# First loads in one queue with the tokens ahead of the adaLN blocks, and two tiles entering the first FFN at once, chunk by chunk

## Chip, cores, metric

One Trainium2 chip, one program on 8 cores (two dies, cores 0 to 3 and 4 to 7). The metric is the device time of the slowest core in microseconds (us). A second, slower state occurs in some executions: one die has a lower granted TensorE clock (the share of its full clock that the chip let TensorE have) and the time is some per cent longer. The ratios leave such runs out and compare fast runs with fast runs; the medians given in us are over all runs of a kernel, so they are only a rough guide.

## The reference, cut to what matters

Two layers of a diffusion backbone. Each sub-layer modulates its input by shift, scale and gate that come out of a matrix product with the conditioning vector (adaLN). The first thing that happens to the tokens is:

```python
mod = silu(cvec) @ ada_w[0] + ada_b[0]             # shift, scale, gate of three sub-layers
h = rms_norm(x, norm_g) * (1 + scale) + shift      # first norm
x = x + 0.5 * gate * ((silu(h @ w1_gate) * (h @ w1_up)) @ w2)
... convolution and attention mixer, FFN; then layer 1 (pooling mixer); final norm
```

Each core has 1280 tokens of width 1024, in tiles 0 and 1 (512 tokens each) and tile 2 (256). So before the first useful matmul a core needs tokens (tile 0: 2 MB), the adaLN blocks for shift and scale (8 of 1 MB) and W1 (22 blocks of 1 MB, gate and up columns side by side).

## The kernel before

A small list scheduler written in Python takes threads of operations, estimates when each could start, and fixes the order on every engine before the program is built. At run time each engine works through its list in that fixed order and waits on semaphores. The ring is a set of buffers through which all weight blocks pass; PSUM banks are the memory that TensorE writes its sums to; the entry is the stretch in which a tile's first W1 matmuls follow its normalisation chunk by chunk (128 channels each). Cuts are marked `...`; comments that explain the code were added here.

```python
IN = [(ACT, True), (DVE, True)] * 4      # squares on ScalarE and VectorE; each summed over channels by an fp32 matmul with ones
A8 = [(ACT, False)] * 8                  # squares on ScalarE, added up on VectorE, ONE fp32 matmul at the end

def xload(self):                         # sync queue
    yield from self.xtile(0, SP)         # tile 0: two loads of 1 MB
    yield self.wait("xin")
    ...                                  # six small loads: finalg, convw, pscale, qkg, amask, cmask

def seq():                               # order of blocks on the GpSimd queue
    for i in range(4):
        yield from ada(0, 4 + i, 5 + i)  # scale block
        yield from ada(0, i, i + 1)      # shift block
    a = list(w1(0, 0))
    yield from a[0:6]
    yield from mix(a[6:], ada(0, 8, 24))
...
for key, src, shape in seq():
    if key in (("w1", 0, 0, 2), ("w1", 0, 0, 3)):
        yield from self.xtile(key[3] - 1, POOL)      # tiles 1 and 2
        self.sigl("xin")
    if key == ("ada", 0, 8):                         # conditioning rows, on the sync queue,
        for v in range(2):                           # into two free slots of the ring: 512 KB each
            ...
            yield self.dma(SP, self.ring[slot[1]][:, :].bitcast(F32),
                           self.d_crow[v:v + 1, :].broadcast_to([128, 1024]), ...)
    ...

# entry of a tile into W1, in ffn(): two W1 blocks (4 PSUM banks), channel chunk by channel chunk
if j == 0 and ("w1", l, s, 1) in self.W:
    ...
    for c in range(8):
        yield self.wait(("h", t, l, i), c + 1)
        yield self.mm([... for q in range(4)], ...)
    ...
norms(1, 0, 0, [IN] * 3)
```

The first eight adaLN blocks are multiplied on TensorE (16 tiny matmuls a block); later ones are dot products on VectorE with the conditioning rows.

The softmax here doesn't subtract the row's maximum and nothing guards it: scores larger than these inputs give would overflow.

## Time and profile before

| | value |
|---|---|
| time, median of 4 runs | 1447.47 us (1446.47 lowest; one slow run of 1593.38) |
| profiled execution | another execution, slow on die 1 (1478.4 us); cores 0 to 3 undisturbed |
| TensorE busy, share of the span | 97% |
| chain that ended last, TensorE's share | 93% |

The cores of the profiled execution of the kernel before: core, span, mean granted clock.

```profile
core 0: 1443.7 us, clock 0.990
core 1: 1439.5 us, clock 0.993
core 2: 1444.4 us, clock 0.994
core 3: 1438.8 us, clock 0.992
...
die 1 (median of its cores): 1472.6 us, clock 0.971
```

Die 1 is in the slow state, so everything below is read from core 0 (or cores 0 to 3).

The chain of waits of core 0 over the first 110 us, in order of time: start, duration, what. This shows what ended the start.

```profile
2.59 33.76 DMA sb_xres<-xin
...
37.14 7.04 PE ps L298 x24
...
51.87 1.38 ACT sb_hbuf L314 x2
53.26 0.53 ACT sb_sq L314
...
53.92 56.16 PE ps L298 x281
```

Tile 0 takes until 36.4 us to arrive.

TensorE of core 0 in the kernel before, in order of time: start, duration, operation, count, and in brackets the idle time before it. `sb_sq,sb_onesf` are the fp32 sums of squares (a matmul appears as two records), `sb_scb` the adaLN matmuls, `sb_hbuf,sb_ring` the W1 matmuls.

```profile
44.00 2.14 PE L298 MATMUL ps<-sb_scb,sb_ring 128*128 128x2 bf16 x80
47.10 5.93 PE L298 MATMUL ps<-sb_hbuf,sb_ring 128*128 128x512 bf16 x20 [0.96 <-issue]
53.92 1.96 PE L298 MATMUL ps<-sb_sq,sb_onesf 128*128 128x512 f32 x4 [0.89 <-ACT sb_sq L314]
...
63.45 12.32 PE L298 MATMUL ps<-sb_hbuf,sb_ring 128*128 128x512 bf16 x56
75.61 1.03 PE L298 MATMUL ps<-sb_sq,sb_onesf 128*128 128x256 f32 x4
```

Between 53.92 and 63.45 us the sums of tile 1 alternate with W1 matmuls of tile 0. At 75.61 us tile 2's fp32 sums begin (8 matmuls of 0.43 us).

### The profile page before, as it was taken

The numbers are of one execution on the slowest core, as the hardware profiler recorded it, in microseconds if no ns is written. First come the engines' busy times: TensorE is split into PE (matmuls) and PEld (weight loads), VectorE is DVE, ScalarE is ACT, GpSimd is POOL, SyncE is SP. The second block draws the span as 40 slices with busy tenths as digits, with TensorE's granted clock in tenths as the row PEclk, the third lists the DMA queues.
The fourth block names the chain that finished last, engine by engine and source line by source line (L and its number), as shares of the span: only waits on it lengthen the run. The fifth ranks groups of instructions, "written<-read, shape, count | busy, mean of one in ns | idle before, by whom it ended". The sixth has DMA issues, their size and how long they took to land.

```text
span 1476.5 us, 21048 instructions; the slowest of 8 cores (1438.8 to 1476.5 us)
## 1 busy us (share of the span) xinstructions
PE 1427.4 (97%) x8578; PEld 774.1 (52%) x8578; DVE 827.6 (56%) x1479; ACT 508.1 (34%) x826; POOL 176.0 (12%) x298
## 2 busy tenths in 40 slices
PE   2899999999999999999999999999999999999997
PEld 0455555457644554555554655555546746555445
DVE  0478861156757998888764478742244862122234
ACT  0651111034399977311123331111133771111111
POOL 3011111334210101111100021100000101000000
PEclk9999999999999999999999999999999999999998
DMA  9999972002629725499750089863221376330012
GB/s 176 215 161 167 151 118 45 15 11 46 99 48 144 116 44 95 74 167 161 119 98 3 1 133 172 152 104 68 44 45 30 55 117 114 59 67 5 1 57 86
DMA packets 42047, 132.19 MB, mean 90 GB/s; under 512 B 6368, under 2 KB 9184, under 8 KB 41952
## 3 DMA queue, kind: packets, MB, share of 16 engines
q0 software_dynamic: 34272, 120.42, 49.2%
q1 hardware_dynamic: 7680, 10.44, 2.3%
q8 instruction: 67, 1.10, 0.3%
q14 instruction: 28, 0.23, 0.1%
HBM read 241.55 MB, written 6.55 MB: 168 GB/s over the span
## 4 chain that ended last, share of the span: by engine, by line
PE 93%; DMA 3%; DVE 1%; ACT 1%; issue 0%; SPq 0%; POOL 0%; DVEq 0%; another core or an unknown queue 0%; ACTq 0%
PE ps L298 93%; DMA sb_xres<-xin 2%; DMA sb_ring<-adaw 1%; DVE sb_nt L319 1%; ACT sb_sg L314 0%; PE ps L307 0%; ACT sb_hbuf L314 0%; ACT sb_areg L314 0%; DVE sb_areg L324 0%; ACT sb_acc L314 0%; DMA yo<-sb_nt 0%; SPq L349 0%; ACT sb_sq L314 0%; DVE sb_xres L319 0%; DVE sb_ring L648 0%
## 5 line engine op out<-in xcount | busy, mean ns | idle before, releaser
L298 PE MATMUL ps<-sb_hbuf,sb_ring 128*128 128x512 bf16 (+1 forms) x4512 | 860.2, 353 | 2.1 <-issue 1.0
L298 PEld LDWEIGHTS ps<-sb_hbuf,sb_ring 128*128 128x128 bf16 x4512 | 446.3, 100 | 391.3 <-issue 89.3
L298 PE MATMUL ps<-sb_areg,sb_ring 128*128 128x512 bf16 (+1 forms) x2304 | 426.1, 345 | 0.0
L314 ACT ACTIVATE sb_sg<-ps 128x512 f32<-128x512 f32 (+3 forms) x279 | 146.1, 528 | 547.2 <-PE ps L298 509.4
L298 PEld LDWEIGHTS ps<-sb_areg,sb_ring 128*128 128x128 bf16 x2304 | 224.3, 98 | 190.8 <-issue 8.3
L324 DVE TENSOR_TENSOR sb_areg<-ps,sb_sg 128x512 bf16<-128x512 f32 (+1 forms) x264 | 157.8, 601 | 297.1 <-PE ps L298 286.8
L319 DVE SCALAR_TENSOR_TENSOR sb_xres<-ps,sb_gsc,sb_xres 128x512 f32<-128x512 f32 (+1 forms) x152 | 96.7, 650 | 165.0 <-PE ps L298 164.4
L648 DVE CUSTOM_DVE_ANT_0 sb_sq<-sb_ring,sb_crow,sb_adab 128x1024 bf16<-128x1024 bf16 x128 | 163.8, 1280 | 23.0 <-DMA sb_ring<-adaw 20.7
L648 DVE CUSTOM_DVE_ANT_0 sb_ring<-sb_ring,sb_crow,sb_adab 128x1024 bf16<-128x1024 bf16 x128 | 163.9, 1280 | 1.9
L314 ACT ACTIVATE sb_sq<-sb_xres 128x512 f32<-128x512 f32 (+1 forms) x123 | 67.9, 558 | 278.7 <-DVE sb_xres L319 217.1
L319 DVE SCALAR_TENSOR_TENSOR sb_nt<-sb_xres,sb_asc,sb_acc 128x512 f32<-128x512 f32 (+1 forms) x144 | 90.5, 664 | 13.8 <-ACT sb_acc L314 10.2
L314 ACT ACTIVATE sb_hbuf<-sb_nt,sb_modsb 128x512 bf16<-128x512 f32 (+1 forms) x136 | 85.4, 659 | 34.0 <-DVE sb_nt L319 33.7
L349 POOL DMA_DIRECT2D sb_ring<-w1t x88 | 47.4, 552 | 349.6 <-PE ps L298 206.4
L324 DVE TENSOR_TENSOR sb_acc<-sb_acc,sb_sq 128x512 f32<-128x512 f32 (+1 forms) x105 | 64.0, 611 | 38.3 <-ACT sb_sq L314 37.7
L349 POOL DMA_DIRECT2D sb_ring<-adaw x72 | 38.7, 540 | 344.1 <-PE ps L298 200.7
L314 ACT ACTIVATE sb_sg<-ps,sb_amask 128x1024 bf16<-128x1024 f32 x67 | 72.7, 1119 | 5.0 <-PE ps L298 4.7
L298 PE MATMUL ps<-sb_areg 128*128 128x65 bf16 (+3 forms) x568 | 60.1, 272 | 3.5 <-ACT sb_sg L314 2.3
L298 PE MATMUL ps<-sb_sq,sb_onesf 128*128 128x512 f32 (+1 forms) x60 | 28.4, 598 | 22.9 <-DVE sb_sq L324 11.5
L349 POOL DMA_DIRECT2D sb_ring<-w2t x44 | 23.3, 529 | 215.1 <-PE ps L298 160.7
L298 PEld LDWEIGHTS ps<-sb_areg 128*128 128x128 bf16 (+1 forms) x568 | 27.8, 95 | 38.9 <-issue 22.8
L218 ACT ACT_TABLE_LOAD x36 | 46.2, 1283 | 1.4 <-PEq L282 0.7
L298 PE MATMUL ps<-sb_ring,sb_hbuf 128*128 128x256 bf16 x320 | 38.6, 276 | 0.2
(75 smaller groups left out, 462.1 us busy)
## 6 DMA issues: line engine op xcount, KB each, us to landing
sb_ring<-w1t POOLq DMA_DIRECT2D x88, 512.0 KB, 13.8
sb_ring<-adaw POOLq DMA_DIRECT2D x72, 512.0 KB, 10.2
sb_ring<-w2t POOLq DMA_DIRECT2D x44, 512.0 KB, 6.3
sb_areg<-mp POOLq DMA_DIRECT2D x5, 512.0 KB, 8.6
sb_xres<-xin SPq DMA_DIRECT2D x2, 1024.0 KB, 26.1
sb_xres<-xin POOLq DMA_DIRECT2D x2, 1024.0 KB, 43.0
sb_ring<-wcx POOLq DMA_DIRECT2D x4, 512.0 KB, 10.9
sb_ring<-wo POOLq DMA_DIRECT2D x4, 512.0 KB, 9.7
```

The costliest lines, as they stand in the source:

```text
L218: eng.preload_act_table_set(ACT_SETS[tab])
L298: ins = e.matmul(m[0], lhsT=m[1], rhs=m[2], start=m[3], stop=m[4], **({"skip_group_check": True} if len(m) > 5 else {}))
L314: o = Op(ACT, lambda e: e.activation(out=out, in_=in_, func=func, **kw), reads, writes, cost)
L319: return Op(DVE, lambda e: e.scalar_tensor_tensor(out=out, in0=in0, scalar=scalar, in1=in1, op0=op0, op1=op1), reads, writes, 150.0 + 1.04 ...
L324: return Op(eng, lambda e: e.tensor_tensor(out=out, in0=in0, in1=in1, op=op), reads, writes, c)
L349: return Op(q, lambda e: e.dma_start(out=out, in_=in_), reads, writes, 600.0 if q == POOL else 450.0, True, nbytes, key)
L648: return Op(DVE, lambda e: e.tensor_tensor_reduce(out=prod, in0=w, in1=self.crow[:, v, :], scale=1.0, scalar=bias, op0=ALU.mult, op1=ALU.a ...
```

## The change

Its intent: all big first loads go into the GpSimd queue in the order of need (tile 0, four adaLN blocks, tile 1, two blocks, W1 0 and 1, two blocks, W1 2, tile 2). Tile 1 enters W1 at the same time as tile 0, in a thread of its own and with one W1 block, so TensorE has matmuls of two tiles while the last adaLN blocks are on their way. Tile 2's squares are added on VectorE.

```diff
     def xload(self):
-        yield from self.xtile(0, SP)
         yield self.wait("xin")
 ...
         def seq():
+            a = list(w1(0, 0))
             for i in range(4):
+                if i == 3:
+                    yield from a[0:2]
                 yield from ada(0, 4 + i, 5 + i)
                 yield from ada(0, i, i + 1)
-            a = list(w1(0, 0))
-            yield from a[0:6]
+            yield from a[2:6]
 ...
+        yield from self.xtile(0, POOL)
         for key, src, shape in seq():
-            if key in (("w1", 0, 0, 2), ("w1", 0, 0, 3)):
-                yield from self.xtile(key[3] - 1, POOL)
+            if key in (("ada", 0, 6), ("w1", 0, 0, 3)):
+                yield from self.xtile(1 if key[0] == "ada" else 2, POOL)
                 self.sigl("xin")
 ...
             if j == 0 and ("w1", l, s, 1) in self.W:
 ...   (the old entry, written in place)
+                nj = 1 if (l, s, t) == (0, 0, 1) else 2
+                room(t, nj - 1)
+                todo[t] += nj
+                if (l, s) == (0, 0):
+                    S.spawn(entry(t, nj), 5.5)      # both tiles at once
+                else:
+                    yield from entry(t, nj)
 ...
+        yield Wait(lambda: not any(left.values()))
         self.sigl(("w1done", l, s))
 ...
-        norms(1, 0, 0, [IN] * 3)
+        norms(1, 0, 0, [IN, IN, A8])
```

The wait before `w1done` makes sure that the entries, now threads of their own, are over. A new field that can delay an operation in the scheduler's estimate is also added, but nothing sets it.

More of the change, by code (lines that the diff above doesn't have):

```diff
@@ L49 @@
     __slots__ = ("eng", "fn", "reads", "writes", "cost", "is_dma", "nbytes", "key", "deps", "marked", "sig", "dval",
-                 "t_end", "tab", "p")
+                 "t_end", "tab", "p", "after")
     def __init__(self, eng, fn, reads, writes, cost, is_dma=False, nbytes=0, key=None):
@@ L58, in __init__ @@
         self.p = None
+        self.after = 0.0
         self.sig = 0
@@ L136, in est @@
     def est(self, o):
-        t = self.free[o.eng]
+        t = max(self.free[o.eng], o.after)
         for d in self.deps_of(o):
@@ L858, in done1, with entry @@
                 self.wfree(("w1", l, s, j))
+        def entry(t, nj):
+            c0, n, v = TILES[t]
+            ks = []
+            for q in range(2 * nj):
+                k = yield from self.bank()
+                ks.append(k)
+            Wv = [self.W[("w1", l, s, q)] for q in range(nj)]
+            for c in range(8):
+                yield self.wait(("h", t, l, i), c + 1)
+                yield self.mm([(self.psv(ks[q], n), Wv[q // 2][0][:, c, 128 * (q % 2):128 * (q % 2) + 128],
+                                self.hbuf[:, c, c0:c0 + n], c == 0, c == 7) for q in range(2 * nj)],
+                              [w[1] for w in Wv] + [self.bh[t][c]], [self.psb[k] for k in ks])
+            for q in range(nj):
+                done1(q)
+                S.spawn(evac(ks[2 * q], ks[2 * q + 1], t, q, n), 1)
         while sum(todo.values()) < 3 * NJ:
@@ L864, in ffn @@
             if j == 0 and ("w1", l, s, 1) in self.W:
-                room(t, 1)
-                todo[t] += 2
-                ks = []
-                for q in range(4):
-                    k = yield from self.bank()
-                    ks.append(k)
-                Wv = [self.W[("w1", l, s, q)] for q in range(2)]
-                for c in range(8):
-                    yield self.wait(("h", t, l, i), c + 1)
-                    yield self.mm([(self.psv(ks[q], n), Wv[q // 2][0][:, c, 128 * (q % 2):128 * (q % 2) + 128],
-                                    self.hbuf[:, c, c0:c0 + n], c == 0, c == 7) for q in range(4)],
-                                  [Wv[0][1], Wv[1][1], self.bh[t][c]], [self.psb[k] for k in ks])
-                for q in range(2):
-                    done1(q)
-                    S.spawn(evac(ks[2 * q], ks[2 * q + 1], t, q, n), 1)
+                nj = 1 if (l, s, t) == (0, 0, 1) else 2
[5 more added lines that the diff above has]
+                    yield from entry(t, nj)
                 continue
```

## The prediction

> What bounds the kernel now. The page gives TensorE 97% of the span, and the chain of waits is 93% TensorE. The profiled run is in the slow state on die 1, so I read cores 0 to 3 (spans 1438.8 to 1444.4 us, clock 0.99). By stretches, TensorE is fully busy from about 75 us on; no wait of it is listed between 100 and 260 us. So only the first 75 us can be shortened; there the DMA share is about 1.0.
>
> The start (transfers' landing, core 2). Token tile 0 comes on the sync queue and shares the engines with eight adaLN blocks on the GpSimd queue: its halves land at 21.9 and 36.2 us; the chain of waits has 33.6 us of that transfer. First FFN matmul 46.1 us. W1 blocks 0 and 1 have landed by 45.7; tile 1 only at 54.4, W1 block 2 at 59.5, block 3 at 68.4 (63.9 to 66.9 on cores 0, 1, 3). Meanwhile TensorE does 48 tile-0 matmuls and tile 1's eight fp32 sums of squares. About 92 to 96 matmuls of tiles 0 and 1 are behind it at 75.6 us (cores 0, 1, 3) and 78.5 us (core 2). Then tile 2's eight fp32 sums take 0.43 us each, 3.4 us.
>
> What the change moves. The Trainium skill ("DMA: Bandwidth & Descriptors", "Issuing engines are not separate DMA queues") says all queues share 16 engines. The trace agrees: while both queues ran, 1 MB of tokens took 14.3 us and an adaLN block (1 MB read) 4.0 us, together 3.1 us per MB; the GpSimd queue alone later took 3.07 us. So one queue makes nothing faster; it reorders: tile 0, four adaLN blocks, tile 1, two blocks, W1 0 and 1, two blocks, W1 2, tile 2, W1 3. The conditioning rows (1 MB) also move from 50-62 us to about 10-20 us, since the sync queue is empty: they delay the early loads by 4 to 5 us.
> Estimate, 5.5 us + 3.1 us per MB + 3 us for rows and small loads: tile 0 at 12 to 15 us, tile 1 near 35, W1 block 0 at 45.5, block 1 at 48.6, last adaLN block 55, W1 block 2 at 58, block 3 at 65. The first matmul comes no earlier, but two tiles are then ready: 36 entry matmuls during 46-55 us, entry done near 59 us after the last adaLN block's normalisation (about 4 us), then 48 matmuls without a wait, 10.3 us. The 96 are done at about 70 us rather than 75.6 to 78.5: 6 to 9 us. Tile 2's sums become one fp32 matmul: 3.0 us. The rest keeps its order, but for small moves in attention, and TensorE-bound time passes the gain to the end. I take 1 us off for evacuations behind table loads or adaLN dot products.
>
> Predicted 1439 us, range 1430 to 1447. Faster by over 2%: 0.02; within 2%: 0.97; slower: 0.01.
>
> What would show it: tile 0 landed by 15 us; W1 block 0 near 45 us; first FFN matmul near 46 us, not earlier; TensorE gapless from about 59 us; one fp32 sum of tile 2; later stages of the same length.
>
> What would make it wrong: early rows cost more; the cold TensorE clock (0.65 to 0.69 in 30-40 us) lasts into the entry; VectorE, 94% busy in 100-180 us, waits for an adaLN block ahead of an evacuation, so banks run out and the lead is given back; most runs in the slow state.

## The result

| | before | changed |
|---|---|---|
| median of 4 runs | 1447.47 us | 1444.09 us |
| lowest, highest (slow) | 1446.47, 1593.38 | 1443.54, 1518.98 |
| ratio of fast runs | | 0.9978 (0.9955 to 1.0000) |

A ratio is the mean time of one kernel's fast runs over that of the other kernel's fast runs of the same rounds, so it is not quite the ratio of the medians. Repeated in five more rounds the changed kernel had 0.9977 (0.9965 to 0.9989). So it gains about 3.3 us (1.6 to 5.1 by that interval) where I forecast about 8.5 (1447.47 to 1439). 1444.09 us lies inside my range, but most of the gain that I named did not come.

The cores of the changed kernel's profiled execution, which was fast:

```profile
core 0: 1435.9 us, clock 0.988
core 1: 1440.1 us, clock 0.988
core 2: 1434.0 us, clock 0.991
core 3: 1437.1 us, clock 0.990
...
core 6: 1442.7 us, clock 0.987
```

The chain of waits of core 0 in the changed kernel, first 110 us:

```profile
5.64 29.42 DMA sb_xres<-xin
...
35.76 10.34 PE ps L299 x32
...
52.80 9.02 PE ps L299 x44
...
61.87 0.77 PE ps L299 x17
...
62.74 0.76 DVE sb_nt L320
...
63.53 0.73 ACT sb_hbuf L315
...
64.30 8.77 PE ps L299 x32
```

It still hangs on a token load, now tile 1's first half (35.05 us). Then comes a stretch in which the last adaLN matmuls (61.87) have to be followed by a normalisation before TensorE can go on at 64.30.

TensorE of core 0 in the changed kernel, in order of time:

```profile
45.92 0.54 PE L299 MATMUL ps<-sb_scb,sb_ring 128*128 128x2 bf16 x16
49.21 1.04 PE L299 MATMUL ps<-sb_hbuf,sb_ring 128*128 128x512 bf16 x3 [2.74 <-ACT sb_hbuf L315]
50.52 0.73 PE L299 MATMUL ps<-sb_hbuf,sb_ring 128*128 128x512 bf16 x2 [0.28 <-ACT sb_hbuf L315]
52.80 6.89 PE L299 MATMUL ps<-sb_hbuf,sb_ring 128*128 128x512 bf16 x20 [1.54 <-ACT sb_hbuf L315]
59.52 0.54 PE L299 MATMUL ps<-sb_scb,sb_ring 128*128 128x2 bf16 x16
59.93 2.32 PE L299 MATMUL ps<-sb_hbuf,sb_ring 128*128 128x512 bf16 x9
62.08 0.54 PE L299 MATMUL ps<-sb_scb,sb_ring 128*128 128x2 bf16 x16
64.30 14.81 PE L299 MATMUL ps<-sb_hbuf,sb_ring 128*128 128x512 bf16 x59 [1.68 <-ACT sb_hbuf L315]
78.95 0.59 PE L299 MATMUL ps<-sb_acc,sb_onesf 128*128 128x256 f32 x2
```

Compare with before. Tile 1's sums are over by 46 us and tile 2 has one sum (78.95). But TensorE, which was without a gap from 53.92 us before, is now without a gap only from 64.30 us. The 20 matmuls from 52.80 us took 6.89 us, 0.34 us each, and some of the 59 from 64.30 us are slow too. The stretches of both kernels say why. Columns: stretch, length, busy us (and count) of PE, PEld, DVE, ACT, POOL, then the granted TensorE clock, DMA share and GB/s. First the kernel before, core 0:

```profile
50.00:60.00 10.00, 9.11 (x32) 3.99 (x31) 4.38 (x10) 4.42 (x7) 0.00 (x0) 1.00 1.03 268
65.00:70.00 5.00, 5.00 (x24) 2.13 (x23) 2.04 (x4) 4.92 (x6) 0.00 (x0) 1.00 1.05 173
```

The same stretches of the changed kernel, core 0:

```profile
50.00:60.00 10.00, 8.19 (x41) 2.99 (x40) 3.40 (x5) 4.08 (x6) 0.00 (x0) 0.66 1.03 184
65.00:70.00 5.00, 5.00 (x18) 1.97 (x17) 1.64 (x4) 4.55 (x7) 0.00 (x0) 0.71 1.04 169
```

The clock is 0.66 and 0.71 where it was 1.00, and 5.00 us of "busy" hold 18 matmuls instead of 24. A TensorE that is shown busy need not be fast.

Landing times are the most useful reading of the start. They are no view of the profile but were worked out from the traces, one profile for each kernel. They are means over cores (0 to 3 for the kernel before, all 8 otherwise), us from the span's start; "end of W1" is the end of the 66th product of the first FFN on VectorE, where all of its W1 work is over:

```
kernel                        tile 0  tile 1  8th adaLN   W1 0  W1 2  rows   9th adaLN   end of
                                              block                   both   block       W1
before                         36.1    53.1     38.3      41.8  58.4  60.5     78.4        251.8
changed                        15.0    39.8     58.7      49.2  61.7  32.5     81.5        249.3
changed, repeated              15.1    38.2     56.9      47.6  59.8  31.3     79.2        248.7
late rows                      14.4    33.5     52.0      42.8  54.7  75.3     78.2        244.1
tile-2 sums alone              36.1    53.3     38.1      41.7  58.4  61.3     79.2        248.2
adaLN blocks first             14.7    38.7     50.8      54.1  60.0  31.4     78.9        247.9
fillers                        15.1    38.0     56.3      47.2  59.4  29.8     78.7        246.2
late rows, fillers             15.3    34.6     53.0      43.8  55.8  76.1     79.0        242.7
late rows, fillers, small late 13.2    32.8     51.4      42.0  54.4  74.7     78.7        241.3
old entry (e5)                 14.9    37.8     56.4      47.1  59.4  31.1     78.4        248.3
old loads, new entry (e6)      36.2    53.9     38.4      42.2  59.0  62.1     79.7        249.9
late rows, old entry (e8)      14.9    33.8     52.7      43.3  55.6  75.7     78.7        244.5
e10                            13.0    32.9     45.2      48.8  54.6  75.0     79.4        242.4
e11                            15.0    34.4     46.7      49.9  55.9  76.2     79.1        243.9
```

The eighth adaLN block is the last that TensorE needs for the first norm. The ninth stands behind the same set of loads in all kernels. It lands at 78.2 to 79.7 us in every profile but one (81.5, the first of the changed kernel): the load order does not change how long all of it takes, only what comes first. And the conditioning rows, which the kernel before first reads at 78.3 us (core 0), have moved from 60.5 to 32 us: with tile 0 gone from the sync queue, nothing held them back any more.

### The profile page after: what moved, and what is told of

It reads as the page before. It is cut to its first block, busy times and chain, and to the rows that moved or that the text cites. A ratio compares the mean times of both kernels' runs of the same rounds, so it can differ in the third digit from the quotient of the medians.

```text
span 1442.7 us, 20898 instructions; the slowest of 8 cores (1434.0 to 1442.7 us)
## 1 busy us (share of the span) xinstructions
PE 1386.4 (96%) x8428; PEld 761.2 (53%) x8564; DVE 827.9 (57%) x1482; ACT 506.9 (35%) x828; POOL 177.7 (12%) x300
## 4 chain that ended last, share of the span: by engine, by line
PE 93%; DMA 3%; DVE 1%; ACT 1%; issue 1%; POOL 0%; DVEq 0%; POOLq 0%; ACTq 0%
PE ps L299 93%; DMA sb_xres<-xin 2%; DMA sb_ring<-adaw 1%; PE ps L308 0%; ACT sb_areg L315 0%; DVE sb_nt L320 0%; DVE sb_areg L325 0%; ACT sb_hbuf L315 0%; POOL sb_ring L350 0%; DVE sb_ring L651 0%; DVE sb_sq L651 0%; DMA yo<-sb_nt 0%; ACT sb_sg L315 0%; ACT sb_acc L315 0%; POOL sb_xres L350 0%
## 5 line engine op out<-in xcount | busy, mean ns | idle before, releaser
L299 PE MATMUL ps<-sb_hbuf,sb_ring 128*128 128x512 bf16 (+1 forms) x4416 | 824.2, 344 | 12.4 <-ACT sb_hbuf L315 6.2
L299 PEld LDWEIGHTS ps<-sb_hbuf,sb_ring 128*128 128x128 bf16 x4512 | 437.9, 98 | 374.4 <-ACT sb_hbuf L315 9.5
L299 PE MATMUL ps<-sb_areg,sb_ring 128*128 128x512 bf16 (+1 forms) x2264 | 420.4, 343 | 2.2 <-DVE sb_areg L325 0.2
L651 DVE CUSTOM_DVE_ANT_0 sb_sq<-sb_ring,sb_crow,sb_adab 128x1024 bf16<-128x1024 bf16 x128 | 163.7, 1279 | 18.1 <-DMA sb_ring<-adaw 17.1
L315 ACT ACTIVATE sb_hbuf<-sb_nt,sb_modsb 128x512 bf16<-128x512 f32 (+1 forms) x136 | 85.2, 656 | 46.3 <-DVE sb_nt L320 45.8
L299 PE MATMUL ps<-sb_sq,sb_onesf 128*128 128x512 f32 (+1 forms) x44 | 23.0, 654 | 15.9 <-ACT sb_sq L315 15.9
## 6 DMA issues: line engine op xcount, KB each, us to landing
sb_ring<-wo POOLq DMA_DIRECT2D x4, 512.0 KB, 11.7
```

Source lines behind the costliest of these rows:

```text
L299: ins = e.matmul(m[0], lhsT=m[1], rhs=m[2], start=m[3], stop=m[4], **({"skip_group_check": True} if len(m) > 5 else {}))
L315: o = Op(ACT, lambda e: e.activation(out=out, in_=in_, func=func, **kw), reads, writes, cost)
L651: return Op(DVE, lambda e: e.tensor_tensor_reduce(out=prod, in0=w, in1=self.crow[:, v, :], scale=1.0, scalar=bias, op0=ALU.mult, op1=ALU.a ...
```

## The experiments

Twelve kernels ran, one of them the changed kernel again. They ran in three groups of four, each group in five rounds on a chip of its own with the kernel before beside it; all ratios are against that kernel before, with their 95% intervals. Two kernels of different groups (e1 and c1, say) are thus compared only by way of it. All edits are to the changed kernel unless said otherwise. All twelve gave correct results. Theory L: the loads are late because the conditioning rows came early. Theory C: TensorE itself, by its halved clock and its fixed order, sets the pace in the entry.

### Late rows (e1_rows_late)

```diff
-                    yield self.dma(SP, self.ring[slot[1]][:, :].bitcast(F32),
+                    yield self.dma(POOL, self.ring[slot[1]][:, :].bitcast(F32),
```

> The changed kernel, but the two conditioning-row loads (1 MB written) are issued on the GpSimd queue behind W1 block 6 instead of on the empty sync queue. Theory L (loads are late because the rows came early): adaLN blocks 1 to 4 land 3.1 us apart instead of 4.0 to 5.2, W1 block 0 lands near 43.5 us instead of 48.3, the last adaLN block near 53.5 instead of 58.3, and the kernel gains 3 to 5 us on the changed one, about 0.9945 of the kernel before. Theory C (TensorE's halved clock and its fixed order set the pace): loads do come earlier, but the last adaLN block's matmuls still start 3 to 4 us after it landed and the first FFN matmuls still run at 427 ns; gain on the changed kernel at most 2 us, 0.997.

Measured: 1437.21 us, ratio 0.9938 (0.9925 to 0.9950). W1 block 0 landed at 42.8 us, the last adaLN block at 52.0, against 47.6 and 56.9 in the repeat of the changed kernel: 4.8 and 4.9 us earlier. The end of W1 came 4.6 us earlier (248.7 to 244.1). Everything on TensorE of core 0 is just shifted:

```profile
49.00 6.93 PE L299 MATMUL ps<-sb_hbuf,sb_ring 128*128 128x512 bf16 x20 [1.62 <-ACT sb_hbuf L315]
55.77 0.54 PE L299 MATMUL ps<-sb_scb,sb_ring 128*128 128x2 bf16 x16
56.17 2.32 PE L299 MATMUL ps<-sb_hbuf,sb_ring 128*128 128x512 bf16 x9
58.33 0.54 PE L299 MATMUL ps<-sb_scb,sb_ring 128*128 128x2 bf16 x16
60.55 14.81 PE L299 MATMUL ps<-sb_hbuf,sb_ring 128*128 128x512 bf16 x59 [1.68 <-ACT sb_hbuf L315]
```

The line of 59 starts at 60.55 instead of 64.30, with much the same 6.93 us for the 20 matmuls ahead. Theory L holds for about 5 us of time. Two later pairs that differ by the late rows repeat it: from e5 to e8 the last adaLN block came 3.7 us earlier (56.4 to 52.7) and the ratio fell from 0.9990 to 0.9957, from e4 to e7 it came 3.3 us earlier (56.3 to 53.0) and the ratio fell from 0.9968 to 0.9941. So the rows cost 3.3 to 4.9 us of load time and 4 to 6 us of time. Theory C's marks stand too: the last adaLN block's matmuls ran 4.9 us after it landed (mean of the cores), and 20 entry matmuls took 6.93 us, as in the changed kernel (6.89). What these cost is not settled by this run; only the loads' share has been removed here.

### Tile-2 sums alone (e2_plan_only)

```diff
-        norms(1, 0, 0, [IN] * 3)
+        norms(1, 0, 0, [IN, IN, A8])       # in the kernel before
```

> The kernel before with only the last line of the change: tile 2's sum of squares is added up on VectorE, so one fp32 matmul takes the place of eight. If those eight (0.43 us each in the trace of before) lie on TensorE's full stretch, this alone gives 3.0 us, ratio 0.998, which would be the whole gain measured for the change; new loads and new entry together would then be worth nothing. If VectorE's extra adds delay evacuations it gives less than 1 us, ratio 0.9995.

Measured: 1444.11 us, ratio 0.9988 (0.9975 to 1.0001). The end of W1 came at 248.2 us against 251.8: 3.6 us by the mean of cores 0 to 3, 2.9 against the three that had no late W1 block (251.1). That is the 3.0 us of the count of matmuls, and as much as the whole change reaches there (248.7). In time it is 1.7 us with an interval from about 0 to 3.6. New loads and new entry together thus show nothing at the end of W1; in time their part is not resolved (0.9988 against 0.9977, with overlapping intervals).

### Blocks first (e3_blocks_first)

```diff
-                if i == 3:
-                    yield from a[0:2]
                 yield from ada(0, 4 + i, 5 + i)
                 yield from ada(0, i, i + 1)
-            yield from a[2:6]
+            yield from a[0:6]
```

> The changed kernel, but all eight adaLN blocks are loaded ahead of W1 blocks 0 and 1, so on TensorE no entry matmul stands before an adaLN matmul. Theory C (fixed order): the wait of 3.8 us between the landing of the last adaLN block and its matmuls goes; the last adaLN block lands near 52 us, W1 block 0 near 55, block 1 near 58; the 48 entry matmuls then run as one burst and are done near 67 us instead of about 69: 1.5 to 3 us faster than the changed kernel, ratio 0.9965. Theory L: nothing gained, since the last of the loads needed lands at the same 58 us: within 1 us of the changed kernel, 0.998.

Measured: 1442.46 us, ratio 0.9975 (0.9963 to 0.9987), the changed kernel's 0.9977. The wait of the last adaLN block's matmuls went from 4.7 us to 0.1 (means of the cores), and the matmuls ran without a gap from here on:

```profile
51.38 0.59 PE L299 MATMUL ps<-sb_scb,sb_ring 128*128 128x2 bf16 x16 [2.14 <-DMA sb_ring<-adaw]
54.58 17.20 PE L299 MATMUL ps<-sb_hbuf,sb_ring 128*128 128x512 bf16 x70 [2.61 <-DMA sb_ring<-w1t]
```

But the wait only moved to the W1 blocks, which now land at 54 us. This order of loads and matmuls is no better than the other. It does not show what TensorE's fixed order costs with the loads left as they were: a run with that order alone changed was not made.

### Fillers (e4_fill)

```diff
         S.spawn(self.main(), 6)
+        S.spawn(self.warm(), 9)
 ...
+    def warm(self):                                   # lowest priority thread
+        rhs = self.onesf[:].bitcast(BF16)
+        while self.S.free[PE] < 62000.0:
+            k = yield from self.bank()
+            yield self.mm([(self.psv(k, 256), self.identb[:], rhs, True, True) for q in range(4)],
+                          [self.b_identb, self.b_onesf], [self.psb[k]])   # never read
+            self.unbank(k)
```

> The changed kernel plus meaningless bf16 matmuls (onesf as data, result never read) wherever the schedule leaves TensorE idle in the first 62 us; all else keeps its order but for single swaps. Theory C (clock): the granted clock stays at 1.0 from about 10 us on, the 20 entry matmuls that took 6.9 us take about 4.4, tile 1's sums take 6 us instead of 9, and the clock loss of 1.8 us at 64 to 68 us goes: 3 to 5 us faster than the changed kernel, ratio 0.995. Theory L (loads alone): no gain, ratio 0.998, or a loss where fillers stand in the way, 1.000.

Measured: 1440.86 us, ratio 0.9968 (0.9956 to 0.9979). Core 0 with fillers, first its stretches, then TensorE:

```profile
50.00:60.00 10.00, 9.87 (x86) 6.06 (x86) 3.07 (x8) 2.10 (x4) 1.06 (x2) 1.00 1.03 220
65.00:70.00 5.00, 4.95 (x24) 2.25 (x23) 3.36 (x8) 2.73 (x8) 0.00 (x0) 1.00 1.03 172
```

```profile
50.21 3.62 PE L299 MATMUL ps<-sb_hbuf,sb_ring 128*128 128x512 bf16 x16
53.66 0.54 PE L299 MATMUL ps<-sb_scb,sb_ring 128*128 128x2 bf16 x16
...
56.65 0.54 PE L299 MATMUL ps<-sb_scb,sb_ring 128*128 128x2 bf16 x16
57.05 2.34 PE L299 MATMUL ps<-sb_onesf,sb_identb 128*128 128x256 bf16 x20
...
73.06 0.59 PE L299 MATMUL ps<-sb_acc,sb_onesf 128*128 128x256 f32 x2
```

The clock is 1.00 throughout, and 16 entry matmuls take 3.62 us, 0.22 each. Tile 2's sum starts at 75.4 us by the mean of the cores, against 78.0 in the repeat of the changed kernel, and W1 ends 2.5 us earlier. Up to 0.6 us of that may be loads that happened to land earlier (last adaLN block 56.3 against 56.9). In time it is 1.3 us (0.9977 to 0.9968), less than the 3 to 5 expected, and the intervals overlap; of the 2.5 us at the end of W1, 1.2 are left in the mean span (1436.3 to 1435.1). Theory C's clock part is shown in the start, at about half the size I gave it; in time it is not clear of the noise.

The Trainium skill ("TensorE: Matmul & The Clock Gate", "What's actually happening") says that after an idle window of about 3.4 us the array runs at half its clock and needs about as long of sustained work to come back. This trace agrees: in the changed kernel the records of the clock on core 0 give 0.5 in stretches of 3.4, 6.8 and 17.1 us, and consecutive W1 matmuls then start 0.43 us apart instead of 0.216.

### The changed kernel again (c1_after_again)

> The changed kernel itself once more, as the common yardstick of these runs: 0.9978 of the kernel before again, within 0.001.

Measured: 1443.57 us, ratio 0.9977 (0.9965 to 0.9989). From tile 1 on its loads landed 1.2 to 2.3 us earlier than in the first profile (tile 0 at the same time), so a difference of 1 to 2 us between two single profiles shows nothing by itself.

### Old entry (e5_loads_plan)

```diff
-                nj = 1 if (l, s, t) == (0, 0, 1) else 2
+                nj = 2
-                if (l, s) == (0, 0):
+                if False:                       # always one tile at a time
```

> The changed kernel with the old entry: one tile at a time with two W1 blocks, tile 1 following after tile 0. If letting two tiles in at once is worth something, this is 2 us or more slower than the changed kernel, ratio 1.000 or above. If the loads' arrival alone sets when TensorE is full (theory L), the entry hardly matters, since the 36 matmuls have to wait for the same last adaLN block: within 1 us of the changed kernel, 0.998.

Measured: 1445.38 us, ratio 0.9990 (0.9977 to 1.0004). It is 1.3 thousandths above the changed kernel, with overlapping intervals, but its W1 ends at 248.3 us, not later than the changed kernel's 248.7. Neither expectation is settled by the ratios.

### Old loads, new entry and sums (e6_entry_plan)

The edit puts the three load hunks of the change back (tile 0 on the sync queue, eight adaLN blocks first, tile 1 ahead of W1 block 2) and keeps the rest.

> The old loads (tile 0 on the sync queue, eight adaLN blocks first, conditioning rows late behind it) with the new entry and the new sums of tile 2. Theory L says the new load order gained nothing because it let the rows in early, so this is as fast as the changed kernel or 1 us faster, 0.9975 to 0.9985, the same as the new sums alone. If the new load order was worth the 6 to 9 us that I forecast for loads and entry, this is 0.9995 or slower.

Measured: 1445.36 us, ratio 0.9995 (0.9981 to 1.0009), a miss: I expected 0.9975 to 0.9985. The new entry with the old loads is no better than the tile-2 sums alone (0.9988), perhaps worse: with the old loads tile 1 arrives at 53.9 us, and there is nothing for a second entry to take in. The end of W1 is at 249.9 us. So the new loads seem to have some worth beside the new entry, 1.8 thousandths (0.9995 to 0.9977, the intervals just overlap), and the new entry shows none without them.

### Late rows and fillers (e7_rows_fill)

The edits of e1 and e4 together, with the fillers ending at 60 us.

> Late rows (0.9938 alone) and fillers (0.9968 alone, 1.5 us below the changed kernel) together. If clock loss and late loads are separate terms they add up: 1435.5 us, ratio 0.993. If earlier loads already leave no idle time the fillers can mend, or if fillers now stand in the way of work that has arrived, no more than the late rows alone: 0.994 or above.

Measured: 1437.31 us, ratio 0.9941 (0.9928 to 0.9954), the late rows alone within the interval. W1 ends 1.4 us earlier than with late rows alone, but the mean span is the same (1431.8 and 1431.9 us): what is left of the fillers' gain is lost later, and I did not find where.

### Late rows, old entry (e8_rows_oldentry)

The edits of e1 and e5 together.

> Late rows with the old entry (one tile at a time). With early rows the new entry was worth 1.3 thousandths against the old one (0.9977 to 0.999). If it is worth the same once the loads are earlier, this is 0.995; if the entry only helps while the last adaLN block is late, this equals the late rows alone, 0.994 or below; if it is worth more now, 0.9965.

Measured: 1440.82 us, ratio 0.9957 (0.9942 to 0.9973). Against the late rows with the new entry (0.9938) it is 1.9 thousandths slower. Together with e5 that is twice the same sign and 1.3 to 1.9 thousandths, so the new entry is probably worth 1 to 3 us; the end of W1 shows none of it (244.5 against 244.1), so where it arises is open.

### Small loads late too (e9_small_late)

On top of e7:

```diff
-        yield self.wait("xin")
+        yield self.wait(("w", ("w1", 0, 0, 6)))
 ...
-            yield self.dma(SP, tl[:], d, [], [b], nb)       # finalg, convw, pscale, qkg, amask, cmask
+            yield self.dma(POOL, tl[:], d, [], [b], nb)
```

> Late rows and fillers (0.9941), and the six small loads of the sync queue, which in the changed kernel ran beside tile 0 (landed 5.5 to 19.6 us), also put behind W1 block 6. If they cost load time as the rows did, tile 0 and the first adaLN blocks land 1 to 2 us earlier and the kernel gains as much: 0.993. If small loads cost nothing: 0.994.

Measured: 1435.75 us, ratio 0.9927 (0.9915 to 0.9940), the fastest of all. Tile 0 landed at 13.2 us instead of 15.3 and the last adaLN block at 51.4 instead of 53.0: six loads of 0.1 MB together had cost 1.6 to 2.1 us of load time. That is no more than two profiles may differ by, but tile 0 landed at 13.0 us in e10 too, and at 14.4 to 15.3 in all nine profiles that have tile 0 first and the small loads early. In time the step from e7 is within the intervals, but W1 ends 1.4 us earlier. This version beats both kernels: about 10.5 us below the one before (0.0073 of 1447) and 7 us below the changed one.

### Blocks first in the best version (e10_blocks_small) and without fillers (e11_blocks_rows)

e10 is e9 with the edit of e3; e11 is e1 with the edit of e3.

> As e9, and all eight adaLN blocks loaded ahead of W1 block 0, so that the normalisation of both tiles is over when W1 block 0 lands near 48 us, and TensorE can run the entry without a stop from W1 block 1 near 51 us. By count of matmuls left this is 0.5 to 2 us better than e9: 0.992. If waiting idle for W1 costs as much as the stops it removes: equal to e9 within 1 us.

Measured: 1437.44 us, ratio 0.9932 (0.9920 to 0.9945), not better than e9.

> Late rows and all adaLN blocks first, no fillers. Against the late rows alone (0.9938) this takes the entry matmuls out of the way of the last adaLN blocks' matmuls (58.33 us for a block that landed at 52.78 in the late-rows run). Fixed order as a cause: 1 to 2 us better, 0.993 or below. No cause: 0.994.

Measured: 1437.39 us, ratio 0.9938 (0.9925 to 0.9950), exactly that of the late rows alone. For the second time loading the adaLN blocks first, so that no entry matmul stands in their way, gained nothing. Of the two orders tried neither is better; that TensorE's fixed order costs nothing is not shown, since the W1 blocks came later with it each time.

## Why the prediction was right or wrong

**Right: what bounds it, and that the queue makes nothing faster.** The gain is small because only the start was shortened: from the end of W1 on, all profiles need much the same, 1187.6 to 1190.2 us (means of the cores). The Trainium skill ("DMA: Bandwidth & Descriptors", "Issuing engines are not separate DMA queues") says that DMAs of all issuing engines run on the same 16 engines and interleave; the runs agree, since the ninth adaLN block lands at 78.2 to 79.7 us in all load orders, apart from one profile at 81.5.

**Right: the rows.** I forecast 4 to 5 us of delay from the conditioning rows coming early. Late rows moved the last adaLN block by 3.3 to 4.9 us in three pairs. (The rows themselves landed at 26 and 31 us on core 0, later than my "about 10-20".) What I failed to see is that this is a side effect worth more than the change itself: removing it alone gained 4 to 6 us in time.

**Right at the end of W1: tile 2's sums.** 3.0 us forecast; 2.9 to 3.6 us at the end of W1 in e2. In time it is 1.7 us with an interval from 0 to 3.6, which neither shows nor excludes the 3.0.

**Right: the first W1 matmul comes no earlier.** It starts at 48.7 to 49.9 us (mean of the cores in two profiles) against 46.3 before, even later than the "near 46" I named.

**Wrong: the entry.** The failed step, in the prediction's words: "36 entry matmuls during 46-55 us, entry done near 59 us after the last adaLN block's normalisation (about 4 us), then 48 matmuls without a wait, 10.3 us. The 96 are done at about 70 us". On core 0 of the changed kernel the 96 were done at 79.0 us, where tile 2's sum begins (78.6 by the mean of the cores, 78.0 in the repeat). The 9 us are three terms of that sum, each read from the trace:

| term | forecast | core 0 | off by |
|---|---|---|---|
| last adaLN block lands | 55 us | 58.3 us | 3.3 |
| its matmuls start after that | at once | 3.8 us later | 3.8 |
| from there to the end of the 96 matmuls | 15 us | 16.9 us (62.1 to 79.0) | 1.9 |

- The first term is loads, and its cause is known only in part. In the three other profiles with this load order and early rows (c1, e4, e5) the block landed at 56.3 to 56.9 us by the mean of the cores, so 1.3 to 1.9 us of it come each time; the first profile was slower (58.7), and why is open. Rows and small loads do not explain it. My formula as printed gives 5.5 + 14 x 3.1 + 3 = 51.9 us, so the 55 us that I named leave about 6 us for them, and the runs show 3.3 to 4.9 us for the rows and 1.6 for the small loads (e9). What was too small is the start of the formula: with neither ahead of it (e9), the block landed at 51.4 us where 5.5 + 14 x 3.1 gives 48.9, and tile 0 at 13.2 us where 5.5 + 2 x 3.1 gives 11.7.
- The second term came from entry matmuls that stand before those of the adaLN blocks in TensorE's fixed list, at half the clock (0.34 us each instead of 0.22). I had the list in front of me and did not cost it. With a full clock the wait shrank from 4.7 to 2.7 us (c1 and e4, means of the cores). But e3 and e11 removed it entirely, by loading W1 later, and gained nothing: the time went into waiting for W1 instead. So this was an error in my account of the entry, and these two runs give no sign that reordering would have got the time back.
- The third term is the clock: the first matmuls after 64.3 us run at half speed because TensorE had stood idle. I listed the cold clock among the things that could make me wrong and gave it nothing. e4 puts all clock effects, those in the second term too, at about 2.5 us at the end of W1; in time 1.3 us, within the noise.

Against these stands a count of the kernel before that was too high. I took 92 to 96 W1 matmuls as done at 75.6 us; the lines show 20 + 3 x 4 + 56 = 88, so the changed kernel is 8 x 0.216 = 1.7 us better off than my comparison. With tile 2's sums (3.0 us) that leaves, on core 0, 75.6 - 79.0 + 1.7 + 3.0 = 1.3 us, and the end of W1 did come 1.4 us earlier there (251.1 to 249.7).

**What remains open.** The split of the measured 3.3 us between the new sums (1.7 us) and the new loads with the new entry (1.6 us) is within the intervals. Why the entry shows in time and not at the end of W1, and why the fillers' lead shrinks after it, is not settled. Both arise after the end of W1: from there to the end of the program it is 1187.6 to 1187.9 us in the changed kernel, its repeat and e1, 1188.8 and 1189.2 with the old entry (e5, e8), and 1188.9 to 1190.2 with fillers (e4, e7, e9), but single cores differ by more than that.

A steadier measure lies in the same runs: the mean span of all eight cores in place of the slowest core. By it (fast runs, 95% intervals worked out from the spans that each run lists) the changed kernel gains 3.4 us on the kernel before (plus or minus 0.8), the new entry is worth 1.3 us (0.7) against e5 on the same chip, and the new loads beside the new entry 2.3 us (1.2) against e6 on the same chip. So both parts are clear of zero; the fillers (0.9 against c1, 0.9) barely are, and blocks first (0.8 against c1, 1.0) and the new sums alone (2.0 against the kernel before, 2.0) are not.

## What to carry to other kernels

Taking a load out of a queue also lets in whatever stood behind it: list what each queue will issue next, and put loads that are not needed yet behind the urgent ones in the same queue. Judge a start by the moment from which the bottleneck engine has no gap and by how much work is still left then, not by how early its first matmul comes; the kernel before had useful work of another kind in the very wait that the change removes. When TensorE is to wait and then run in short bursts, count those matmuls at the slow rate that the trace shows (here 0.34 to 0.43 us each instead of 0.216).

## What the Trainium skill lacked or had wrong

- "TensorE: Matmul & The Clock Gate": the halved clock and its 3.4 us windows are as stated (0.5 in multiples of 3.4 us, matmuls 0.43 us apart). The page says the ramp is under 1% of a typical span, which holds here (1.3 us of 1444, itself within the noise), but that would be some 40% of the gain in question. It has no number for fillers in a start that waits for loads: here they gave 2.5 us at the end of the first W1 and 1.3 us in time (intervals overlap), and nothing in time once the rows were late (0.9941 against 0.9938).
- "DMA: Bandwidth & Descriptors": that issuing engines share the 16 DMA engines holds, but that section does not say what follows for order. The page describes elsewhere how an engine takes turns between queues, without a measured case like this one: an emptied sync queue let 1 MB of unneeded rows interleave with urgent loads, and the last adaLN block landed 3.3 to 4.9 us later.
- The same page says why small descriptors are slow, but does not say what a few small loads cost the large ones beside them: six loads of 0.1 MB in all moved the tokens by 2.1 us and the last adaLN block by 1.6 us.
